# Linear attention's scores on one Trainium2 core: high and low key parts stacked on the rows, two products in place of three

## The chip, the cores and the metric

One core of a Trainium2 chip runs the whole program. The metric is the device time of one execution in microseconds (us), lower is better. TensorE does the matrix products, VectorE (DVE), ScalarE (ACT) and GpSimd (POOL) the work on elements, and SyncE (SP) issues the transfers.

## What is computed

A two-layer encoder on 512 tokens of 1024 channels, all in 32-bit floats. A layer normalizes the stream, projects it once, feeds three mixers (attention, a long convolution, gated linear attention), merges them with gates, and adds a cross-attention and an MLP. The change touches the linear attention alone: four heads, keys and queries of 64 channels, values of 128, one scan forward and one backward. The part of the reference that matters:

```
q_dec = q * jnp.exp(b)
a = jnp.einsum("bhncd,bhnsd->bhncs", q_dec, k * jnp.exp(-b))
mask = jnp.tril(jnp.ones((C, C), dtype=bool), k=0 if include_diag else -1)
o = jnp.einsum("bhncs,bhnse->bhnce", jnp.where(mask, a, 0.0), v)
...
o_f = gla_scan(q, k, v, g_f, True)
o_b = fl(gla_scan(fl(q), fl(k), fl(v), fl(g_b), False))
```

The scores `a` of both directions are what the change computes in another way.

## The kernel before, in words

**Products in three parts.** TensorE takes its operands in a rounded 32-bit format (F32R). To keep precision, `split` (L234 to L237) makes of every operand a high part, by a cast on ScalarE (L235), and a low part, by a subtraction on VectorE (L236); `mm3` (L249 to L253) then adds three products into one accumulator: high by high (L251), high by low (L252), low by high (L253).

**Layout of the heads.** For each head, one tile `qd` and one tile `kd` of 128 rows by 512 tokens hold the decayed queries and keys: rows 0 to 63 are the forward direction, rows 64 to 127 the backward one. They come from `gla_proj`, and `gla_heads` (L997) works through the heads in order, in three steps for each: the scores; the states; the output.

**The scores.** `gla_heads` splits `qd` and `kd` (two casts of 128x512 on ScalarE, two subtractions on VectorE), takes for each direction `d` the row half `rr`, and for each of four tiles of 128 tokens calls `mm3` on 64 rows: keys are the weights, queries move. That is 3 x 4 x 2 = 24 products a head, each with 64 rows of weights and 128 columns. The two directions use opposite halves of the rows of the array and write two accumulators. Direction 0 is then copied to `A` by ScalarE (L1019), direction 1 laid over it under a mask by VectorE (L1021).

**Order.** The text of the program is woven from generators by a list of step names (`ORDER0`, `ORDER`); each instruction has a priority by its place there, and `late("gA")` sets the score products back by 100. A planner then fixes the order on every engine before the run, with buffers handed out from pools (`g`: 13 in this phase, `st`: 6). So between the score products of a head there can stand products of other work: wide ones (128x512) of the projections, and transposes.

**Names in the rows.** `qdh`, `qdl`, `kdh`, `kdl` are the high and low parts; `ps` is an accumulator; `Ah`, `Sh` scores and states; `osq` squares of a head's output; `wh`, `wl`, `xh`, `xl` weights and stream of the projections. In the changed kernel the stacked tiles are named `k2` and `q2`, which lists show as `k` and `q`.

Of the kernel before, what the change touches and what calls it, by code (L numbers as in the profile page):

```python
# [10 lines left out]
F32 = mybir.dt.float32  # L11
F32R = mybir.dt.float32r
# [3 lines left out]
ALU = mybir.AluOpType  # L16
# [158 lines left out]
class Trunk:  # L175
# [821 lines left out]
    def gla_heads(self, l):  # L997
        nc, W = self.nc, self.I["w_in"][l]
        self.yc = []
        for h in range(4):  # L1000
# [1 line left out]
            tiles = lambda ap: ap.rearrange("p (t s) -> p t s", s=P)  # L1002
            per_tile = lambda ap: ap.unsqueeze(2).to_broadcast([P, NT, P])
            qh, ql = self.split_new(self.qd[h], "g", name="qd")
            kh, kl = self.split_new(self.kd[h], "g", name="kd")
            vh, vl = self.split_new(self.vf[h], "g", (P, NT, P), "v", lo_eng=nc.gpsimd)
            k3 = self.t("st", name="k3")
            nc.gpsimd.tensor_tensor(tiles(k3), tiles(self.kd[h]), per_tile(end), op=ALU.mult)
# [2 lines left out]
            for d in range(2):  # L1011
                rr = slice(64 * d, 64 * d + 64)
                ps = self.ps("a", (P, NT, P))
                for t in range(NT):
                    tk = slice(t * P, (t + 1) * P)
                    with self.late("gA"):
                        self.mm3(ps[:, t], kh[rr, tk], kl[rr, tk], qh[rr, tk], ql[rr, tk], True, True)
                if d == 0:
                    nc.scalar.copy(A, ps)  # L1019
                else:  # L1020
                    nc.vector.copy_predicated(A, self.mask.unsqueeze(1).to_broadcast([P, NT, P]), ps)  # L1021
# [3 lines left out]
            ps = self.ps("a", (P, NT, P))  # L1025
# [37 lines left out]
            for t in range(NT):  # L1063
                tk = slice(t * P, (t + 1) * P)
# [399 lines left out]
```

## Time and profile before

| what | value |
|---|---|
| median of 3 runs | 2220.78 us (2219.13 to 2222.26) |
| the profiled execution's own time | 2222.39 us |
| its span | 2220.6 us |
| TensorE busy | 2176.5 us, 98% of the span |
| VectorE, ScalarE, GpSimd busy | 68%, 46%, 9% |
| granted TensorE clock, mean | 0.992 of full speed |
| score products | 192 of 10968 TensorE products |

The busy time of TensorE is a union of overlapping records (a product's record is longer than the step to the next), so what one product takes is read from the starts in the timeline. Around the span lie 1.8 us of the execution.

### The profile page before, as it was taken

To read this page: it belongs to the slowest core of one execution; us is meant where nothing else is said; L and a number is where in the kernel's file an instruction comes from. 1 tells how busy PE (TensorE), PEld (TensorE's weight loads), DVE (VectorE), ACT (ScalarE), POOL (GpSimd) and SP (SyncE) were. 2 spreads that over 40 slices of the span, in tenths; PEclk is the share of its full clock that TensorE was granted. 3 is DMA by queue.
4 is the path that set the end of the run, shared out by engine and by line. 5 is a ranking of instruction groups with operands and counts; after the bars stand their busy time and mean duration, and the time that the engine had idled before them with its cause. 6 is when DMAs were issued, how large, how long until landed. Compare 5 with 4: busy or idle time off the path is not lost.

```text
span 2220.6 us, 28780 instructions
## 1 busy us (share of the span) xinstructions
PE 2176.5 (98%) x10968; PEld 1822.2 (82%) x10968; DVE 1517.3 (68%) x2539; ACT 1015.9 (46%) x1711; POOL 203.3 (9%) x193
## 2 busy tenths in 40 slices
PE   7999999999999999999999999999999999999999
PEld 5878888888788878888887978888887888888887
DVE  7699955869866756776485686657897575344445
ACT  6666845433344544443336477453434454332231
POOL 2030001000010200000060130100000101000004
PEclk9999999999999999999999999999999999999999
DMA  6442123233243333333344311342233312333332
GB/s 234 147 135 88 65 77 119 60 102 114 86 137 101 95 110 121 125 117 95 97 166 131 109 57 47 97 128 76 81 110 124 133 58 86 95 96 104 95 99 92
DMA packets 80098, 233.56 MB, mean 105 GB/s; under 512 B 9174, under 2 KB 11222, under 8 KB 79960
## 3 DMA queue, kind: packets, MB, share of 16 engines
q1 hardware_dynamic: 76792, 225.95, 31.9%
q0 software_dynamic: 3168, 5.77, 1.0%
q8 instruction: 86, 1.41, 0.3%
q14 instruction: 52, 0.43, 0.1%
HBM read 214.91 MB, written 16.78 MB: 104 GB/s over the span
## 4 chain that ended last, share of the span: by engine, by line
PE 75%; DVE 3%; ACT 2%; DMA 1%; issue 1%; POOL 0%; ACTq 0%; DVEq 0%; POOLq 0%
PE ps L251 24%; PE ps L253 24%; PE ps L252 24%; DVE wl L236 1%; ACT wh L235 1%; DMA wr<-in_w_in_dram 1%; PE ps L1318 0%; PE ps L555 0%; PE ps L793 0%; PE ps L543 0%; PE ps L564 0%; ACT p L547 0%; ACT pth L235 0%; PE ps L1276 0%; DVE ab L966 0%
## 5 line engine op out<-in xcount | busy, mean ns | idle before, releaser
L236 DVE TENSOR_TENSOR wl<-wr,wh 128x1024 fp32r<-128x1024 f32 x324 | 402.3, 1243 | 265.8 <-ACT wh L235 258.5
L235 ACT CAST wh<-wr 128x1024 fp32r<-128x1024 f32 (+1 forms) x328 | 341.6, 1043 | 512.1 <-PE ps L252 413.4
L253 PE MATMUL ps<-xh,wl 128*128 128x512 f32 x1344 | 530.9, 396 | 9.0 <-DVE wl L236 9.0
L251 PE MATMUL ps<-xh,wh 128*128 128x512 f32 x1344 | 533.3, 397 | 2.0 <-ACT wh L235 1.6
L252 PE MATMUL ps<-xl,wh 128*128 128x512 f32 x1344 | 529.4, 394 | 0.0
L253 PEld LDWEIGHTS ps<-xh,wl 128*128 128x128 f32 x1344 | 254.9, 190 | 63.9 <-DVE wl L236 12.3
L251 PEld LDWEIGHTS ps<-xh,wh 128*128 128x128 f32 x1344 | 254.7, 190 | 56.6 <-ACT wh L235 2.9
L252 PEld LDWEIGHTS ps<-xl,wh 128*128 128x128 f32 x1344 | 254.8, 190 | 49.7
L253 PE MATMUL ps<-hdh,wl 128*128 128x512 f32 x512 | 199.4, 390 | 0.0
L252 PE MATMUL ps<-hdl,wh 128*128 128x512 f32 x512 | 199.4, 390 | 0.0
L251 PE MATMUL ps<-hdh,wh 128*128 128x512 f32 x512 | 199.2, 389 | 0.0
L1380 DVE TENSOR_TENSOR macc<-ps,macc 128x512 f32<-128x512 f32 x96 | 66.3, 690 | 85.4 <-PE ps L253 84.8
L253 PEld LDWEIGHTS ps<-hdh,wl 128*128 128x128 f32 x512 | 96.1, 188 | 19.9
L251 PEld LDWEIGHTS ps<-hdh,wh 128*128 128x128 f32 x512 | 96.1, 188 | 19.8
L252 PEld LDWEIGHTS ps<-hdl,wh 128*128 128x128 f32 x512 | 96.1, 188 | 19.8
L352 POOL TENSOR_TENSOR hsum<-hsum,hsq 128x512 f32<-128x512 f32 x30 | 43.4, 1446 | 582.9 <-ACT hsq L350 582.9
L252 PE MATMUL ps<-wl,xh 128*128 128x256 f32 x320 | 91.6, 286 | 1.0 <-DVE wl L236 0.9
L251 PE MATMUL ps<-wh,xh 128*128 128x256 f32 x320 | 91.5, 286 | 0.1
L253 PE MATMUL ps<-wh,xl 128*128 128x256 f32 x320 | 90.9, 284 | 0.0
L1364 DVE TENSOR_TENSOR rl<-rl 128x512 f32<-128x512 f32 x64 | 44.0, 688 | 63.4 <-ACT rl L1363 63.4
L1382 POOL TENSOR_TENSOR macc<-macc,rb 128x512 f32<-128x512 f32 x16 | 23.5, 1469 | 651.2 <-DVE macc L1380 651.2
L1363 ACT ACTIVATE rl<-ps 128x512 f32<-128x512 f32 x64 | 37.9, 592 | 77.9 <-PE ps L253 77.9
(403 smaller groups left out, 4309.1 us busy)
## 6 DMA issues: line engine op xcount, KB each, us to landing
wr<-in_mlp_w_dram SPq DMA_DIRECT2D x128, 512.0 KB, 3.6
wr<-in_w_in_dram SPq DMA_DIRECT2D x108, 512.0 KB, 3.7
wraw<-in_x_wv_dram SPq DMA_DIRECT2D x16, 512.0 KB, 5.5
wr<-in_x_wk_dram SPq DMA_DIRECT2D x16, 512.0 KB, 3.6
F<-ff SPq DMA_DIRECT2D x32, 256.0 KB, 2.9
F<-F SPq DMA_DIRECT2D x32, 256.0 KB, 4.8
wr<-in_w_out_dram SPq DMA_DIRECT2D x16, 512.0 KB, 3.6
wr<-in_x_wq_dram SPq DMA_DIRECT2D x16, 512.0 KB, 3.7
```

The costliest lines, as they stand in the source:

```text
L235: r = self.nc.scalar.copy(hi, src)
L236: (lo_eng or self.nc.vector).tensor_tensor(lo, src, hi, op=ALU.subtract)
L251: mm(out, lh, rh, start=start, stop=False, skip_group_check=True)
L252: mm(out, lh, rl, start=False, stop=False, skip_group_check=True)
L253: mm(out, ll, rh, start=False, stop=stop, skip_group_check=True)
L352: eng.tensor_tensor(self.hsum, self.hsum, sq, op=ALU.add)
L1363: nc.scalar.activation(r, ps, AF.Relu)
L1364: nc.vector.tensor_tensor(r, r, r, op=ALU.mult)
L1380: nc.vector.tensor_tensor(acc[m], ps, acc[m], op=ALU.add)
L1382: nc.gpsimd.tensor_tensor(acc[m], acc[m], rb, op=ALU.mult)
```

## The change

For each head and each direction `d`, a tile `kk` of 128 rows is made: the rows of the direction (`r`) hold the high part of the keys, the other half (`o`) their low part. A tile `qq` holds the high part of the queries twice, once in each half. One product of 128 rows then gives high by high plus low by high; a second product, of the 64 rows `r` alone, adds high keys by low queries. The queries' own split is kept, since their parts are used again behind.

On ScalarE the one cast of the keys (128x512) becomes, for each direction, one cast of 64x512 for the keys and two of 64x512 for the queries' copies; on VectorE the one subtraction (128x512) becomes two of 64x512. The tiles `kk` take the two `g` buffers of the old parts; the tiles `qq` take two more `st` buffers a head.

```diff
--- before.py
+++ after.py
@@ -1002,7 +1002,18 @@
             tiles = lambda ap: ap.rearrange("p (t s) -> p t s", s=P)
             per_tile = lambda ap: ap.unsqueeze(2).to_broadcast([P, NT, P])
             qh, ql = self.split_new(self.qd[h], "g", name="qd")
-            kh, kl = self.split_new(self.kd[h], "g", name="kd")
+            kd, K2, Q2 = self.kd[h], [], []
+            for d in range(2):
+
+                r, o = slice(64 * d, 64 * d + 64), slice(64 - 64 * d, 128 - 64 * d)
+                kk = self.t("g", dt=F32R, name="k2")
+                nc.scalar.copy(kk[r], kd[r])
+                nc.vector.tensor_tensor(kk[o], kd[r], kk[r], op=ALU.subtract)
+                K2.append(kk)
+                qq = self.t("st", dt=F32R, name="q2")
+                for x in (r, o):
+                    nc.scalar.copy(qq[x], qh[r].bitcast(F32))
+                Q2.append(qq)
             vh, vl = self.split_new(self.vf[h], "g", (P, NT, P), "v", lo_eng=nc.gpsimd)
             k3 = self.t("st", name="k3")
             nc.gpsimd.tensor_tensor(tiles(k3), tiles(self.kd[h]), per_tile(end), op=ALU.mult)
@@ -1014,7 +1025,10 @@
                 for t in range(NT):
                     tk = slice(t * P, (t + 1) * P)
                     with self.late("gA"):
-                        self.mm3(ps[:, t], kh[rr, tk], kl[rr, tk], qh[rr, tk], ql[rr, tk], True, True)
+                        nc.tensor.matmul(ps[:, t], K2[d][:, tk], Q2[d][:, tk], start=True, stop=False,
+                                         skip_group_check=True)
+                        nc.tensor.matmul(ps[:, t], K2[d][rr, tk], ql[rr, tk], start=False, stop=True,
+                                         skip_group_check=True)
                 if d == 0:
                     nc.scalar.copy(A, ps)
                 else:
```

Three places in the planned order. The first is TensorE, scores of head 2 in layer 0, before (`qdh`/`qdl` with `kdh`/`kdl`: 64 rows each; `ps_3558` is direction 0, on the first half of the rows, `ps_3572` direction 1, on the second):

```order
L1087 MATMUL ps_3533<-consts,oy_3528 128x128
L251 MATMUL ps_3558<-qdh_3543,kdh_3547 128x128
L252 MATMUL ps_3558<-qdl_3544,kdh_3547 128x128
L251 MATMUL ps_3572<-qdh_3543,kdh_3547 128x128
L253 MATMUL ps_3558<-qdh_3543,kdl_3548 128x128
L251 MATMUL ps_3558<-qdh_3543,kdh_3547 128x128
L252 MATMUL ps_3558<-qdl_3544,kdh_3547 128x128
L252 MATMUL ps_3572<-qdl_3544,kdh_3547 128x128
L253 MATMUL ps_3558<-qdh_3543,kdl_3548 128x128
L251 MATMUL ps_3558<-qdh_3543,kdh_3547 128x128
L252 MATMUL ps_3558<-qdl_3544,kdh_3547 128x128
```

and of the change (L1028 is the stacked product, 128 rows; L1030 the second one, 64 rows):

```order
L1101 MATMUL ps_3533<-consts,oy_3528 128x128
L1028 MATMUL ps_3566<-q_674_3550,k_673_3547 128x128
L1030 MATMUL ps_3566<-qdl_3544,k_673_3547 128x128
L1028 MATMUL ps_3566<-q_674_3550,k_673_3547 128x128
L1028 MATMUL ps_3576<-q_676_3556,k_675_3553 128x128
L1030 MATMUL ps_3566<-qdl_3544,k_673_3547 128x128
L1028 MATMUL ps_3566<-q_674_3550,k_673_3547 128x128
L1030 MATMUL ps_3566<-qdl_3544,k_673_3547 128x128
L1028 MATMUL ps_3566<-q_674_3550,k_673_3547 128x128
L1030 MATMUL ps_3566<-qdl_3544,k_673_3547 128x128
L1030 MATMUL ps_3576<-qdl_3544,k_675_3553 128x128
L1028 MATMUL ps_3576<-q_676_3556,k_675_3553 128x128
```

Before, all 24 products of this head stand together and have 64 rows; now products of 128 and of 64 rows take turns. Counted over the eight groups of scores in the order of TensorE, the height changes 36 times before (8, 2, 2, 4, 10, 4, 2, 4 times, entry and exit of a group included) and 114 times now (14 times in each group, 16 in one).

The second place is ScalarE at the split of head 1 in layer 0 (`A` is the copy of the scores), before:

```order
L235 CAST Sh_3231<-S_3208 128x512
L235 CAST qdh_3327<-qk_100_522 128x512
L235 CAST kdh_3331<-qk_115_694 128x512
L235 CAST vh_3335<-vf_2879 128x512
L1073 ACTIVATE osq_3322,small<-ps_3297 128x128 x4
L1019 COPY A_3341<-ps_3342 128x512
```

and of the change:

```order
L235 CAST Sh_3231<-S_3208 128x512
L235 CAST qdh_3327<-qk_100_522 128x512
L1010 CAST k_638_3331<-qk_115_694 64x512
L1010 CAST k_640_3337<-qk_115_694 64x512
L235 CAST vh_3343<-vf_2879 128x512
L1087 ACTIVATE osq_3322,small<-ps_3297 128x128 x4
L1015 CAST q_639_3334<-qdh_3327 64x512 x2
L1015 CAST q_641_3340<-qdh_3327 64x512 x2
L1033 COPY A_3349<-ps_3350 128x512
```

The copies of the queries stand behind the squares of head 0's output now. On TensorE the scores of head 1, which stood ahead of all but one of that output's products, now stand behind them and ten wide products more. In layer 1 the copies stand behind the squares too, and the scores behind ten wide products.

The third place is VectorE where head 0 of layer 1 is prepared, before:

```order
L236 TENSOR_TENSOR qdl_12299<-qk_1693_10387,qdh_12298 128x512
L973 TENSOR_TENSOR ab_11134<-ab_11134,small 128x512
L236 TENSOR_TENSOR kdl_12303<-qk_1699_10455,kdh_12302 128x512
L531 TENSOR_TENSOR ql_11162<-ps_11156,qh_11161 64x512
L982 SCALAR_TENSOR_TENSOR qk_1697_10421<-qk_1697_10421,mn_11153 128x512
```

and of the change:

```order
L236 TENSOR_TENSOR qdl_12299<-qk_1701_10387,qdh_12298 128x512
L973 TENSOR_TENSOR ab_11134<-ab_11134,small 128x512
L1011 TENSOR_TENSOR k_2012_12302<-qk_1707_10455,k_2012_12302 64x512
L1011 TENSOR_TENSOR k_2014_12308<-qk_1707_10455,k_2014_12308 64x512
L531 TENSOR_TENSOR ql_11162<-ps_11156,qh_11161 64x512
```

One more subtraction stands ahead of the attention's `ql`.

## Rows read from the trace of the kernel before

**Rows 1.** The page, parts 1 and 4: busy time of each engine with its share of the span and its count of instructions; and the chain that ended last, by engine.

```profile
PE 2176.5 (98%) x10968; PEld 1822.2 (82%) x10968; DVE 1517.3 (68%) x2539; ACT 1015.9 (46%) x1711; POOL 203.3 (9%) x193
...
PE 75%; DVE 3%; ACT 2%; DMA 1%; issue 1%; POOL 0%; ACTq 0%; DVEq 0%; POOLq 0%
```

**Rows 2.** The groups of TensorE instructions by line and form: the first of the three groups of score products (the other two, on L252 and L253, have the same 64 instructions and form). Columns: line, engine, operation, tiles, weights' rows*columns, moving rows x columns, count | busy us, mean ns of one | idle us before.

```profile
L251 PE MATMUL ps<-qdh,kdh 64*128 64x128 f32 x64 | 15.3, 294 | 0.7 <-ACT kdh L235 0.7
```

**Rows 3.** The timeline of TensorE in layer 0, the scores of head 2, with transposes of other work ahead and behind. Columns: start us, duration us, engine, line, operation, tiles, form, count of merged instructions. 'x2' is two products whose starts fall together, one of each half of the rows.

```profile
382.65 0.60 PE L1087 MATMUL ps<-consts,oy 128*128 128x128 f32 x4
383.17 0.33 PE L251 MATMUL ps<-qdh,kdh 64*128 64x128 f32 x2
383.34 0.33 PE L252 MATMUL ps<-qdl,kdh 64*128 64x128 f32 x2
383.45 0.27 PE L253 MATMUL ps<-qdh,kdl 64*128 64x128 f32 x1
383.56 0.27 PE L251 MATMUL ps<-qdh,kdh 64*128 64x128 f32 x1
...
384.12 0.33 PE L253 MATMUL ps<-qdh,kdl 64*128 64x128 f32 x2
384.23 0.33 PE L251 MATMUL ps<-qdh,kdh 64*128 64x128 f32 x2
384.34 0.33 PE L252 MATMUL ps<-qdl,kdh 64*128 64x128 f32 x2
384.46 0.33 PE L253 MATMUL ps<-qdh,kdl 64*128 64x128 f32 x2
...
385.19 0.27 PE L253 MATMUL ps<-qdh,kdl 64*128 64x128 f32 x1
385.39 0.44 PE L1028 MATMUL ps<-consts,k 128*128 128x128 f32 x2
```

**Rows 4.** The same view in layer 1, the scores of head 0, with wide products (128x512) of other work between them.

```profile
1391.30 0.39 PE L251 MATMUL ps<-wh,mnh 128*128 128x512 f32 x1
1391.52 0.39 PE L252 MATMUL ps<-wl,mnh 128*128 128x512 f32 x1
1391.84 0.32 PE L251 MATMUL ps<-qdh,kdh 64*128 64x128 f32 x1
1392.09 0.50 PE L253 MATMUL ps<-wh,mnl 128*128 128x512 f32 x1
1392.53 0.33 PE L251 MATMUL ps<-qdh,kdh 64*128 64x128 f32 x1
1392.78 0.66 PE L1028 MATMUL ps<-consts,k 128*128 128x128 f32 x4
...
1393.95 0.50 PE L251 MATMUL ps<-wh,mnh 128*128 128x512 f32 x1
1394.38 0.32 PE L253 MATMUL ps<-qdh,kdl 64*128 64x128 f32 x1
1394.55 0.27 PE L251 MATMUL ps<-qdh,kdh 64*128 64x128 f32 x1
```

**Rows 5.** Busy time by stretch: from:to, its length, busy us and count of each engine, then the granted TensorE clock (1.00 is 2.4 GHz, 0.50 is 1.2 GHz), the DMA share and GB/s. The first row spans the scores of head 0 of layer 0; the third begins inside those of head 1.

```profile
301.30:306.00 4.70, 4.70 (x32) 3.69 (x31) 1.82 (x2) 2.16 (x3) 0.00 (x0) 1.00 0.59 197
306.00:309.40 3.40, 3.40 (x9) 2.72 (x9) 2.32 (x5) 1.10 (x2) 0.00 (x0) 0.50 0.11 41
...
326.50:336.70 10.20, 10.20 (x48) 9.49 (x47) 0.19 (x1) 1.84 (x10) 1.32 (x2) 0.50 0.01 2
...
383.00:1302.70 919.70, 909.86 (x4480) 759.46 (x4478) 649.91 (x1083) 400.36 (x627) 91.72 (x82) 1.00 0.35 111
...
1309.50:2214.00 904.50, 901.08 (x4496) 754.09 (x4495) 567.88 (x883) 371.49 (x626) 62.30 (x46) 1.00 0.30 94
```

**Rows 6.** The timeline of TensorE behind the scores of head 0, layer 0: two wide products in a row.

```profile
307.02 0.63 PE L253 MATMUL ps<-xh,wl 128*128 128x512 f32 x1
307.45 0.63 PE L251 MATMUL ps<-xh,wh 128*128 128x512 f32 x1
```

**Rows 7.** Groups of ScalarE instructions by line and form, columns as in Rows 2: the keys' high part now, and a cast of 64 rows of 512 from the same memory.

```profile
L533 ACT CAST ql<-ql 64x512 fp32r<-64x512 f32 x16 | 9.9, 618 | 0.8 <-DVE ql L531 0.3
...
L235 ACT CAST kdh<-qk 128x512 fp32r<-128x512 f32 x8 | 4.9, 616 | 0.0
```

**Rows 8.** The timeline of TensorE at the scores of head 1, layer 0; in brackets the idle time before, and what ended it.

```profile
324.87 0.33 PE L251 MATMUL ps<-qdh,kdh 64*128 64x128 f32 x2 [0.73 <-ACT kdh L235]
...
325.76 0.32 PE L253 MATMUL ps<-qdh,kdl 64*128 64x128 f32 x1 [0.28 <-DVE kdl L236]
```

**Rows 9.** The timeline of ScalarE there: the squares of head 0's output (four with their sums), and the copy behind them.

```profile
334.86 0.28 ACT L1073 ACTIVATE osq<-ps 128x128 f32<-128x128 f32 x1 [9.53 <-PE ps L253]
...
335.88 0.60 ACT L1019 COPY A<-ps 128x512 f32<-128x512 f32 x1
```

**Rows 10.** The timeline of TensorE where head 0 of layer 1 is prepared: the longest single wait in that stretch.

```profile
1303.97 1.22 PE L543 MATMUL ps<-k,ql 128*128 128x512 f32 x2 [3.29 <-ACT ql L533]
```

**Rows 11.** The timeline of VectorE there: the keys' low part, and the low part of the attention's queries behind it.

```profile
1301.87 0.68 DVE L236 TENSOR_TENSOR kdl<-qk,kdh 128x512 fp32r<-128x512 f32 x1
1302.59 0.68 DVE L531 TENSOR_TENSOR ql<-ps,qh 64x512 fp32r<-64x512 f32 x1
```

**Rows 12.** Busy time by stretch, columns as in Rows 5: where head 0 of layer 0 is prepared.

```profile
140.00:180.00 40.00, 36.69 (x168) 29.79 (x167) 39.60 (x77) 22.12 (x41) 11.40 (x14) 0.97 0.39 123
```


## The prediction, as it was made before the changed kernel ran

> **What bounds the kernel now.** I read the page first: TensorE is busy 98% of the span and is 75% of the chain that ended last, every other engine far behind [rows 1]. So what lengthens or shortens TensorE's own line of work goes nearly whole into the time, and what the other engines get added costs only where TensorE waits for them. The page counts records that overlap, so the price of a product is not its mean of 294 ns [rows 2] but the step from its start to the next start, and that is in the timeline.
>
> Three things are to be seen in the scores of one head [rows 3]. Within a run of 64-row products the step is 0.11 us (383.45 to 383.56). Where "x2" stands, two products start together, one on each half of the rows: their line holds two products in a step of 0.11. And from the last 64-row product to the first 128-row one the step is 0.20 us (385.19 to 385.39), with no wait named: 0.09 is lost on the way out. The other way it is the same, and the first step after a change is 0.16 to 0.17 in place of 0.11 (383.17 to 383.34; 1394.38 to 1394.55) [rows 3, 4]. So a run of products of one height costs 0.11 for each, and 0.05 at its beginning and 0.09 at its end: **0.14 us for each change of height**. A product alone between two changes shows it at once: 0.25 us, 1391.84 to 1392.09 and 1392.53 to 1392.78 [rows 4]. A wide product alone between two changes takes 0.44 and 0.43, and 0.22 in a run (1391.30 to 1391.52): 0.2 on top [rows 4].
>
> **The products themselves.** Three groups of 64 [rows 2] become two: 64 products fewer, at 0.11 a step, -7.0 us.
>
> **The changes of height.** The stacked product has 128 rows, the one after it 64, and the planned order lets them take turns: 114 changes for 36, 78 more at 0.14, +10.9 us.
>
> **The shared time.** A 128-row product uses both halves, so it cannot start together with another. In the group of head 2 that is lost: 24 products at 0.11, plus 0.14 for the two changes' parts that lie within, would be 2.78 us, and from 383.17 to 385.39 it takes 2.22 [rows 3], 0.56 less. I take 0.5 for each of eight groups, +4.0 us. Back comes what the order still leaves: in most groups one 64-row product of each direction stands side by side, 0.11 each, -0.9 us.
>
> Together +7.0 us on TensorE. As a whole: now 192 x 0.11 - 4.0 + 36 x 0.14 = 22.2 us, then 128 x 0.11 - 0.9 + 114 x 0.14 = 29.1 us, or 2.8 and 3.6 us a head. No row shows a 128-row product of 128 columns alone between two changes. From above it is bounded by the wide one, which pays 0.2 where the narrow 64-row one pays 0.14 [rows 4]: 0.06 more for six or so a head, eight heads, +2.9 us, so 9.9. From below, a change could cost nothing in the new order: then 14.1 us in place of 22.2, -8.1. I take 0.14, since it is the row of the nearest form, the same columns and the same two changes.
>
> The Trainium skill has a rule on each side. TensorEngine Tiling (Array Packing), section Key Properties, says that changing the tiling mode, not just the tile, drains TensorE; it gives no price, and the trace agrees, with 0.20 in place of 0.11 at each change. TensorE: Matmul & The Clock Gate, section LDWEIGHTS (loading the stationary operand), says that a weight load goes by its columns and that a 32-row one takes as long as a 128-row one. By that rule alone rows are free, and the change is a gain of its 64 products; it stands beside the first rival below.
>
> **The clock.** The granted clock is 0.50 right behind the scores of head 0 in layer 0, for 3.4 us, and again from within those of head 1, for 10.2 us [rows 5]; at that level a wide product takes 0.43 in place of 0.22 [rows 6], so half of each stretch is lost: 6.8 us of the 13.6. It stays at 1.00 for all other groups (the long stretches from 383.0 and from 1309.5) [rows 5]. Both falls came at groups that were broken up by changes or held up by waits [rows 5, 8]; one more group as broken up, that of head 0 in layer 1 [rows 4], had none: two of three. Every group is broken up like that after the change and lasts 3.6 us, so I take falls at six of eight, 3.4 us each: 20.4 us at half clock for 13.6, +3.4 us. The ends: none at all, -6.8; all eight, one of them as long as now, 34.0 for 13.6, +10.2.
>
> **ScalarE and VectorE.** One cast of 616 ns becomes six of 64x512, and a cast of that form takes 618 [rows 7], so rows don't shorten it: 40 more in all, 25 us on an engine that is free for half of the span [rows 1]. They are hidden wherever a split stands well ahead of its scores, which is so for all heads but head 1. There TensorE now waits 0.73 us for a cast and 0.28 for a subtraction [rows 8]. The new order moves these scores behind head 0's output, which takes that wait away, -1.0 us. But the copies of the queries stand behind the squares, which take 1.0 us from 334.86 to 335.88 [rows 9], and two casts are 1.2 more, while TensorE has ten wide products, 2.2 us, to do meanwhile. That is even; with the hand-over from engine to engine, which is not in it, I put 0.3 us of wait in both layers, +0.6. In layer 1, TensorE waits 3.29 us for the attention's `ql` [rows 10], whose subtraction follows the keys' low part on VectorE at once [rows 11]. Two subtractions of 64 rows stand there now; these take 0.68 each (a 64-row one is the row of `ql` itself), so the wait grows by 0.6 us. Where head 0 of layer 0 is split, VectorE is busy 39.60 of 40 us and TensorE only 36.69 [rows 12], so one more subtraction is worth up to 0.6 there too. Sum +0.8; between -1.0, if none of the waits comes, and +3, if all casts of head 1 hold TensorE up. No transfer is added or moved past another by the change itself; the two more `st` buffers a head are used and free again within a head. The planner also reorders rows elsewhere; I price that at nothing and allow 3 us each way, about the longest single wait that I cite.
>
> **The sum.** 7.0 + 3.4 + 0.8 = +11.2 us. On the profiled execution's 2222.39 that is 2233.6; that execution lies 1.6 above the median of the runs shown, 2220.78, against which I forecast **2232.0 us**, slower by 0.5%. With the bounds of each part its own range is 2226 to 2241.
>
> **The rivals.**
> First, the change of height is paid for only by what stands now, where products of other work come between, and is hidden when the same accumulator goes on: the next weights load behind the product that runs. For it: steps of 0.11 within a run hide the loads already [rows 3]. Against it: the same 0.20 stands at every change, between all kinds of neighbours [rows 3, 4]. Then the scores take 14.1 us, -8.1, with the waits' +0.8 and the clock as now: 2213.5 us, **faster**. It decides at 0.08 us a change: there 128 x 0.11 - 0.9 + 114 x 0.08 is the 22.2 of now. Chance 0.14. In the Trainium skill, the columns-only rule of TensorE: Matmul & The Clock Gate, cited above, speaks for this rival.
> Second, the falls of the clock go away, since half of the products now fill all 128 rows: 7.0 - 6.8 + 0.8 = +1.0, 2221.8 us, **no difference**. For it: six of eight groups have no fall now [rows 5]. Against it: the groups get longer and more broken up. Chance 0.16.
> Third, the casts become the bound: at head 1 of both layers TensorE waits for five more casts, 3.1 us each at 0.62 [rows 7], 6.2 us for the 0.6 above: 2237.6 us. It would be seen as a wait for a cast ahead of the first stacked product. Against it: ten wide products stand between. Chance 0.08.
>
> **How the numbers follow.** The forecast has 0.62. What a measurement of this kernel can tell from no change is about 0.2%, 4.4 us. Slower by more: forecast and third rival, 0.70. Within: the second, 0.16. Faster by more: the first, 0.14. The range runs from 2219, which takes in the second rival with 3 us for the order elsewhere, to 2241; it leaves out the first rival and a little at the top.
>
> **What would show it.** In the profile after: stacked and 64-row products in turn with steps of 0.25 us, no "x2" but for side-by-side 64-row ones; 3.6 us from the first to the last of a group; a granted clock of 0.50 right behind most groups; the wait of 0.73 at head 1 gone and the wait for `ql` at some 3.9 us. Wrong would be steps of 0.11 across the two forms (the first rival), or no stretch at 0.50 between 300 and 420 us (the second). More than 1 us of wait ahead of a stacked product would speak for the third.

## The result, and the profile of the changed kernel

The changed kernel takes 2238.52 us (median of four runs, 2236.58 to 2243.68), the kernel before beside it 2220.94. The ratio is 1.0085, with a 95% interval of 1.0071 to 1.0099: slower by 17.6 us, 0.8%. The forecast was 2232.0 in a range of 2219 to 2241. The profiled execution took 2238.0 us, its span is 2236.2: 15.6 longer than the span before.

The page, parts 1 and 4, answers to [rows 1]. TensorE has 64 products fewer and is busy 10.8 us longer; the chain is still its own line of work.

```profile
PE 2187.3 (98%) x10904; PEld 1827.4 (82%) x10904; DVE 1528.3 (68%) x2547; ACT 1041.7 (47%) x1751; POOL 199.0 (9%) x193
...
PE 87%; DVE 6%; ACT 4%; DMA 1%; issue 1%; POOL 0%; SPq 0%; ACTq 0%; DVEq 0%; POOLq 0%
```

The groups of score products by line and form answer to [rows 2]: columns as there. The means, 317 and 331 ns, are again lengths of overlapping records; that they rose by a tenth says little beside the steps that follow.

```profile
L1028 PE MATMUL ps<-q,k 128*128 128x128 f32 x64 | 19.3, 317 | 0.3 <-ACT q L1015 0.3
L1030 PE MATMUL ps<-qdl,k 64*128 64x128 f32 x64 | 18.9, 331 | 0.0
```

The timeline of TensorE at the scores of head 2 in layer 0 answers to [rows 3]: start us, duration us, engine, line, tiles, form, count of merged instructions.

```profile
382.39 0.30 PE L1028 MATMUL ps<-q,k 128*128 128x128 f32 x1
382.62 0.32 PE L1030 MATMUL ps<-qdl,k 64*128 64x128 f32 x1
382.87 0.44 PE L1028 MATMUL ps<-q,k 128*128 128x128 f32 x2
383.24 0.32 PE L1030 MATMUL ps<-qdl,k 64*128 64x128 f32 x1
383.50 0.33 PE L1028 MATMUL ps<-q,k 128*128 128x128 f32 x1
383.75 0.32 PE L1030 MATMUL ps<-qdl,k 64*128 64x128 f32 x1
384.00 0.33 PE L1028 MATMUL ps<-q,k 128*128 128x128 f32 x1
384.26 0.33 PE L1030 MATMUL ps<-qdl,k 64*128 64x128 f32 x2
384.52 0.33 PE L1028 MATMUL ps<-q,k 128*128 128x128 f32 x1
...
385.81 0.32 PE L1030 MATMUL ps<-qdl,k 64*128 64x128 f32 x1
386.06 0.33 PE L1042 MATMUL ps<-consts,k 128*128 128x128 f32 x1
```

Read the starts: 383.24, 383.50, 383.75, 384.00, 384.26, 384.52. Each product, of 128 rows or of 64, takes 0.25 to 0.26 us, though none waits; before, the step was 0.11. Where two of one kind follow each other (x2 at 382.87), they take 0.37 together, 0.12 more than one; the x2 at 384.26 is a pair of opposite halves and costs no more than one product. The group takes 3.67 us (382.39 to 386.06) for 16 products, where 24 took 2.22.

Busy time by stretch answers to [rows 5]: from:to, length, busy us and count of PE, PEld, DVE, ACT, POOL, then the granted clock (1.00 is 2.4 GHz, 0.50 is 1.2), DMA share, GB/s.

```profile
302.20:306.00 3.80, 3.80 (x21) 2.70 (x19) 1.82 (x2) 2.11 (x3) 0.00 (x0) 0.99 0.57 161
306.00:309.40 3.40, 3.40 (x9) 2.71 (x9) 2.16 (x4) 1.10 (x2) 0.00 (x0) 0.50 0.34 134
326.40:329.80 3.40, 3.40 (x12) 2.82 (x12) 0.99 (x2) 3.15 (x12) 2.50 (x2) 0.51 0.00 0
...
411.80:415.20 3.40, 3.40 (x15) 3.17 (x16) 2.50 (x4) 1.41 (x3) 0.00 (x0) 0.50 0.00 0
...
1401.60:1405.00 3.40, 3.40 (x10) 2.62 (x9) 1.86 (x5) 1.10 (x2) 0.00 (x0) 0.51 0.15 61
...
1428.90:1435.70 6.80, 6.80 (x17) 5.30 (x17) 2.32 (x5) 1.10 (x2) 0.00 (x0) 0.50 0.13 51
...
1514.30:1517.70 3.40, 3.40 (x16) 3.21 (x16) 3.24 (x6) 1.69 (x3) 0.00 (x0) 0.50 0.00 0
```

The first two rows are one event: a group of alternating products, TensorE busy without a gap and at 0.99, and then 3.4 us at 0.50. Five of the eight groups are followed by such a stretch, one of them of 6.8 us. The row at 326.40 stands just ahead of the scores of head 1.

The timeline of TensorE at its waits answers to [rows 8, 10]; brackets give the idle time and what ended it.

```profile
324.71 0.33 PE L251 MATMUL ps<-Sh,qdh 128*128 128x128 f32 x1 [0.78 <-ACT Sh L235]
325.44 0.33 PE L252 MATMUL ps<-Sl,qdh 128*128 128x128 f32 x1 [0.40 <-DVE Sl L236]
...
330.66 0.22 PE L1028 MATMUL ps<-q,k 128*128 128x128 f32 x1
...
1303.87 0.73 PE L542 MATMUL ps<-k,qh 128*128 128x512 f32 x2 [1.89 <-ACT qh L530]
...
1309.22 1.03 PE L543 MATMUL ps<-k,ql 128*128 128x512 f32 x2 [3.02 <-ACT ql L533]
```

The first scores of head 1 start without a wait (330.66), but the waits they had, 0.73 and 0.28, now stand ahead of head 0's output, whose products take the early place: 0.78 and 0.40. In layer 1 a wait of 1.89 us is new. The timeline of ScalarE shows what the attention's `qh` stood behind: a step (L975) that itself waited 1.13 us for VectorE, and the two casts of the keys, 1.25.

```profile
1300.17 0.63 ACT L975 ACTIVATE mn<-ab 128x512 f32<-128x512 f32 x1 [1.13 <-DVE ab L973]
...
1301.38 1.25 ACT L1010 CAST k<-qk 64x512 fp32r<-64x512 f32 x2
1302.65 1.17 ACT L530 CAST qh<-ps 64x512 fp32r<-64x512 f32 x2
```

### The profile page after: what moved, and what is told of

It is laid out like the page before. It is cut to its first block, busy times and chain, and to the rows that moved or that the text cites. A ratio compares the mean times of both kernels' runs of the same rounds, so it can differ in the third digit from the quotient of the medians.

```text
span 2236.2 us, 28707 instructions
## 1 busy us (share of the span) xinstructions
PE 2187.3 (98%) x10904; PEld 1827.4 (82%) x10904; DVE 1528.3 (68%) x2547; ACT 1041.7 (47%) x1751; POOL 199.0 (9%) x193
## 4 chain that ended last, share of the span: by engine, by line
PE 87%; DVE 6%; ACT 4%; DMA 1%; issue 1%; POOL 0%; SPq 0%; ACTq 0%; DVEq 0%; POOLq 0%
PE ps L251 27%; PE ps L252 27%; PE ps L253 27%; DVE wl L236 1%; DMA wr<-in_w_in_dram 1%; ACT wh L235 1%; PE ps L555 1%; ACT p L547 1%; PE ps L1030 1%; PE ps L1028 1%; PE ps L564 1%; PE ps L542 0%; ACT pth L235 0%; PE ps L566 0%; PE ps L543 0%
## 5 line engine op out<-in xcount | busy, mean ns | idle before, releaser
L253 PE MATMUL ps<-xh,wl 128*128 128x512 f32 x1344 | 530.7, 395 | 7.3 <-DVE wl L236 7.3
L252 PE MATMUL ps<-xl,wh 128*128 128x512 f32 x1344 | 529.5, 395 | 0.0
L253 PEld LDWEIGHTS ps<-xh,wl 128*128 128x128 f32 x1344 | 254.8, 190 | 62.0 <-DVE wl L236 10.3
L252 PEld LDWEIGHTS ps<-xl,wh 128*128 128x128 f32 x1344 | 255.1, 190 | 50.4
L253 PE MATMUL ps<-hdh,wl 128*128 128x512 f32 x512 | 199.6, 390 | 0.0
L252 PE MATMUL ps<-hdl,wh 128*128 128x512 f32 x512 | 199.6, 390 | 0.0
L253 PEld LDWEIGHTS ps<-hdh,wl 128*128 128x128 f32 x512 | 96.2, 188 | 19.8
L252 PEld LDWEIGHTS ps<-hdl,wh 128*128 128x128 f32 x512 | 96.2, 188 | 19.7
L252 PE MATMUL ps<-wl,xh 128*128 128x256 f32 x320 | 91.4, 286 | 0.4 <-DVE wl L236 0.4
L253 PE MATMUL ps<-wh,xl 128*128 128x256 f32 x320 | 91.4, 286 | 0.0
L1378 DVE TENSOR_TENSOR rl<-rl 128x512 f32<-128x512 f32 x64 | 44.1, 688 | 62.4 <-ACT rl L1377 62.4
```

The costliest lines, as they stand in the source:

```text
L252: mm(out, lh, rl, start=False, stop=False, skip_group_check=True)
L253: mm(out, ll, rh, start=False, stop=stop, skip_group_check=True)
L1378: nc.vector.tensor_tensor(r, r, r, op=ALU.mult)
```

## The experiments

For every profiled execution I take the span apart in the same way. *Idle* is the span less TensorE's busy time. *Half clock* is the sum of all stretches at 0.50 up to TensorE's last product, of which I take half as lost. What is left, the *rest*, holds the score products (all else is the same work), and is given as the difference to before. Beside it stands what the prediction's two prices give: 0.11 us a step, 0.14 a change of height. For the change the sum closes: +15.6 = 4.8 idle + 1.7 clock + 9.1 rest.

| kernel | median us | ratio to before (95%) | idle us | half clock us | changes of height | rest us | by the two prices |
|---|---|---|---|---|---|---|---|
| before | 2220.94 | 1 | 44.1 | 37.5 | 36 | 0 | 0 |
| the change | 2238.52 | 1.0085 (1.0071 to 1.0099) | 48.9 | 41.0 | 114 | +9.1 | +7.0 |
| e1 heights apart | 2225.64 | 1.0025 (1.0014 to 1.0037) | 54.6 | 30.7 | 26 | -4.1 | -8.0 |
| e2 halves paired | 2213.84 | 0.9964 (0.9949 to 0.9978) | 47.9 | 23.9 | 18 | -9.2 | -9.1 |
| e4 all of 128 rows | 2218.04 | 0.9988 (0.9978 to 0.9997) | 51.5 | 23.9 | 0 | -6.4 | -8.1 |
| e5 late pairs | 2246.93 | 1.0117 (1.0100 to 1.0134) | 46.4 | 75.1 | 118 | +5.2 | +7.7 |
| e3 casts alone | 2230.24 | 1.0049 (1.0034 to 1.0064) | 49.7 | 37.5 | 40 | +1.8 | +0.6 |
| e7 before, early | 2227.01 | 1.0036 (1.0024 to 1.0047) | 48.0 | 51.2 | 18 | -4.5 | -2.6 |
| e8 change, early | 2243.78 | 1.0110 (1.0091 to 1.0129) | 49.2 | 51.2 | 116 | +5.9 | +7.2 |
| e9 no copies | 2239.45 | 1.0082 (1.0062 to 1.0102) | 46.3 | 58.0 | 112 | +3.7 | +6.7 |
| e10 pairs in place | 2217.26 | 0.9990 (0.9980 to 0.9999) | 49.6 | 30.7 | 20 | -10.3 | -8.8 |

Each ratio is against runs of the kernel before on the same chip. The three columns in us are each of one execution, and the clock scatters most between executions. The mean granted clock of each execution was taken, too; 1 less that clock, times the span, estimates what the clock costs. For the change this is 24.6 us on average (four executions, 22.4 to 29.1), for the kernel before 16.0 to 17.4 (13 to 23 executions on each of three chips). By this estimate the clock is about 7 us of the change's 17.6, and not 1.7, and idle time and rest together are about 11, not 13.9.

My theory: the change of height costs, and takes more than the saved products give. Rivals: the 128-row form itself is dear, the casts are, or the place of the scores in the order is.

**e1: the same products, sorted by height.** All eight stacked products of a head first, then the eight of 64 rows, halves in turn, and the group kept together.

```diff
-            for d in range(2):
-                rr = slice(64 * d, 64 * d + 64)
-                ps = self.ps("a", (P, NT, P))
+            pss = [self.ps("a", (P, NT, P)) for d in range(2)]
+            with self.tc.high_priority(offset=1000):
+                for d in range(2):
...
+                        nc.tensor.matmul(pss[d][:, t], K2[d][:, tk], Q2[d][:, tk], start=t == 0, stop=False, ...)
...
+                    for d in range(2):
+                        rr = slice(64 * d, 64 * d + 64)
+                        nc.tensor.matmul(pss[d][:, t], K2[d][rr, tk], ql[rr, tk], start=False, stop=t == NT - 1, ...)
```

> The change's casts, tiles and products, in another order: for a head all eight stacked products first, then the eight 64-row ones with the two halves of the rows in turn, and high priority so that they stay together. 26 changes of height in the planned order in place of 114. Theory (each change of height costs 0.14 us on TensorE): 10.6 us of steps + 26 x 0.14 = 14.2 us for all scores in place of 29.1, so 15 us under the change: some 2223, and less if falls of the clock behind the groups go away too (down to 2213). Rival (the added casts and the waits they bring are the cost, changes of height are free): no other than the change, 2238 within 3.

The timeline of TensorE at one head:

```profile
378.35 1.09 PE L1027 MATMUL ps<-q,k 128*128 128x128 f32 x8
379.37 0.66 PE L1033 MATMUL ps<-qdl,k 64*128 64x128 f32 x8
379.96 0.33 PE L1047 MATMUL ps<-consts,k 128*128 128x128 f32 x1
```

The 16 products that took 3.67 us take 1.61, so neither form is dear in itself; only their taking turns is. The rest fell by 13.2 us against the change (15.0 by the prices: some groups kept waits and foreign products within them), and the whole by less, as TensorE idles 5.7 us more. The place was changed along with the sorting; e8 below tells these apart.

**e4: the change with no change of height.** The low queries too are copied into both halves, so the second product has 128 rows (high and low keys by low queries), at the price of four more subtractions a head.

```diff
+                ll = self.t("st", dt=F32R, name="l2")
+                for x in (r, o):
+                    nc.vector.tensor_tensor(ll[x], self.qd[h][r], qh[r], op=ALU.subtract)
+                L2.append(ll)
...
-                        nc.tensor.matmul(ps[:, t], K2[d][rr, tk], ql[rr, tk], start=False, stop=True,
+                        nc.tensor.matmul(ps[:, t], K2[d][:, tk], L2[d][:, tk], start=False, stop=True,
```

> The change in its own loop order, but the second product has 128 rows too: the low part of the queries is laid in both halves as well (four more 64x512 subtractions a head on VectorE), so the product adds low by low to what is asked for. As many products as the change, no change of height. Theory: 128 x 0.11 = 14.1 us for the scores in place of 29.1: 15 us under the change, 2223, some 1 to 3 us more for the subtractions, less for falls of the clock that go away. Rival (casts and their waits): 2238 or above, as more is added.

The same view of head 2:

```profile
373.54 0.28 PE L1034 MATMUL ps<-l,k 128*128 128x128 f32 x1
373.65 0.28 PE L1032 MATMUL ps<-q,k 128*128 128x128 f32 x1
373.76 0.27 PE L1034 MATMUL ps<-l,k 128*128 128x128 f32 x1
```

This is the cleanest trial: the same number of products as the change, more rows in half of them, more work on VectorE, and steps of 0.11 in place of 0.25. The rest is -6.4 us where the prices say -8.1, and the time 20.5 us under the change: of the 21.4 us of span between the two profiles, 15.5 are the rest and 8.5 the clock, and idle time takes 2.6 back. The priority of the products was left as it is; the planner still moved them in places (13 products of other work stand within the group of head 3 in layer 0, where the change has 4). The Trainium skill, TensorE: Matmul & The Clock Gate, section LDWEIGHTS (loading the stationary operand), says that rows don't matter to a weight load; these steps agree with it, within one height.

**e2: the old products, opposite halves side by side.** Before's 24 products and its split, the two directions in turn, kept together.

```diff
+            pss = [self.ps("a", (P, NT, P)) for d in range(2)]
+            with self.tc.high_priority(offset=1000):
...
+                    for i, (kx, qx) in enumerate(((kh, qh), (kh, ql), (kl, qh))):
+                        for d in range(2):
+                            rr = slice(64 * d, 64 * d + 64)
+                            nc.tensor.matmul(pss[d][:, t], kx[rr, tk], qx[rr, tk], start=i == 0, stop=i == 2, ...)
```

> The kernel before with its own 24 products of 64 rows a head, ordered so that direction 0 and direction 1 always follow each other, kept together by high priority: 18 changes of height (36 before). Theory: 96 shared steps x 0.11 + 18 x 0.14 = 13.1 us in place of 22.2, 9 us under the kernel before: 2212, and down to 2205 if the falls of the clock at the groups go. If products of opposite halves did not really run side by side: no more than the 18 changes, 2.5 us, so 2218.

The same view:

```profile
375.19 0.28 PE L1018 MATMUL ps<-qdl,kdh 64*128 64x128 f32 x2
375.31 0.27 PE L1018 MATMUL ps<-qdh,kdl 64*128 64x128 f32 x2
375.42 0.28 PE L1018 MATMUL ps<-qdh,kdh 64*128 64x128 f32 x2
...
1291.84 0.47 PE L1018 MATMUL ps<-qdl,kdh 64*128 64x128 f32 x2 [3.88 <-DVE qdl L236]
```

Every line of head 2 is a pair, and the steps are 0.12 and 0.11: 24 products in 1.48 us, against 2.22 in [rows 3]. Two products of opposite halves cost one. It is the fastest version that ran, 0.36% under before. Its early place makes TensorE wait 3.88 us for head 0 of layer 1, with the clock at 0.50 behind that wait. This is no loss against before: the wait of 3.29 for the attention's `ql` [rows 10] is gone from that stretch, and before, too, stood at 0.50 there for 6.8 us (1302.7 to 1309.5).

**e5: the same pairs, late.** The priority of e2 replaced by the one that before and the change use, so that wide products of other work come between.

```diff
-            with self.tc.high_priority(offset=1000):
+            with self.late("gA"):
```

> The products and tiles of the run with paired halves, but with the low priority of the kernel before: the planner then puts wide products between the pairs of the first head of each layer, 118 changes of height in place of 18. No cast or tile is added to the kernel before. Theory (change of height): 100 changes more at 0.14 to 0.2 us, 14 to 20 us above the run with paired halves, 2 to 8 us above the kernel before. Rival (changes of height are free, casts cost): the same time as the run with paired halves, within 2 us.

The timeline of TensorE at head 0, at full and at half clock, and the stretches at half clock:

```profile
303.09 0.50 PE L252 MATMUL ps<-xl,wh 128*128 128x512 f32 x1
303.52 0.33 PE L1018 MATMUL ps<-qdl,kdh 64*128 64x128 f32 x1
303.78 0.51 PE L253 MATMUL ps<-xh,wl 128*128 128x512 f32 x1
...
310.12 0.47 PE L1018 MATMUL ps<-qdh,kdh 64*128 64x128 f32 x1
310.52 0.79 PE L253 MATMUL ps<-xh,wl 128*128 128x512 f32 x1
311.25 0.47 PE L1018 MATMUL ps<-qdh,kdh 64*128 64x128 f32 x1
...
309.10:326.10 17.00, 17.00 (x33) 9.55 (x34) 1.46 (x3) 2.18 (x4) 0.00 (x0) 0.50 0.00 0
1408.20:1428.70 20.50, 20.50 (x44) 11.68 (x44) 2.03 (x3) 3.62 (x8) 0.00 (x0) 0.50 0.12 45
```

Here no product has the stacked form, there is no added cast, and yet this is the slowest kernel: 26 us above before, where I had put 2 to 8. The wide products stand between the two halves of a pair, too, so a 64-row product and a wide one take turns, 0.69 us for both (303.09 to 303.78, next wide product) in place of 0.33. That is 118 changes of height and 25 steps more than in e2, +7.7 by the prices; the rest is +5.2 us.

The clock gives +18.8 more by the table's rule. The stretches of 17.0 and 20.5 us begin within the groups of head 0, which start at 301.3 and 1403.2, and outlast them: the turns go on until 322.9 and 1425.4. At half clock two products in turn take 1.13 us (310.12 to 311.25), less than twice 0.69, so some 3 us of the 18.8 belong to the rest (an estimate from these two steps). So turns of height cost with other products than the change's, too; but most of the loss here is the clock, which the two prices don't hold.

**e3: the change's casts, before's products.** Keys cast and subtracted in halves, the four copies made and not used, `mm3` on 64 rows kept.

```diff
+            kh, kl = (self.t("g", dt=F32R, name="k2") for _ in range(2))
...
+                nc.scalar.copy(kh[r], kd[r])
+                nc.vector.tensor_tensor(kl[r], kd[r], kh[r], op=ALU.subtract)
...
+                        self.mm3(ps[:, t], kh[rr, tk], kl[rr, tk], qh[rr, tk], ql[rr, tk], True, True)
```

> The change's work on the other engines, without its products: six casts and three subtractions a head as in the change (the high parts of the keys by halves, the copies of the queries, which nothing reads here), the two more st buffers a head, and then the 24 products of 64 rows of the kernel before. 40 changes of height in the planned order (36 before). Theory (changes of height cost, casts are hidden): the kernel before and the 0.8 us of waits and 0.6 of changes, 2220 to 2224. Rival (the casts and their waits are most of the 17.6 us): 2232 or above.

The timeline of TensorE at head 1 of layer 0, and the clock behind it:

```profile
323.71 0.32 PE L251 MATMUL ps<-qdh,k 64*128 64x128 f32 x1 [1.93 <-ACT k L1009]
...
324.50:338.10 13.60, 13.60 (x52) 11.75 (x52) 3.06 (x7) 5.50 (x16) 2.37 (x2) 0.50 0.00 1
```

My theory missed: I had put 2220 to 2224, and it is 11 us slower than before with almost the same steps. The scores of head 1 stand directly behind the key casts here, the waits of 0.73 and 0.28 [rows 8] become one of 1.93, and 13.6 us at half clock follow, for 10.2 in [rows 5]. The table puts 5.6 of its 7.4 us of span into idle time. Of these, 0.9 are that wait, and 2.7 stand between 138 and 300 us, where layer 0 is prepared: TensorE idles 7.9 us there for 5.2 before. So the casts and subtractions are not free; in the change they are hidden at head 1, since its scores start without a wait (330.66 above), but not between 138 and 300 us, where it idles 7.8.

**e9: the change without the copies.** `Q2` is `qh` itself, so 32 casts and the two `st` buffers a head fall away. Left out is the copy of the high queries into the other half, so the stacked product multiplies the low keys by the other direction's queries.

```diff
-                qq = self.t("st", dt=F32R, name="q2")
-                for x in (r, o):
-                    nc.scalar.copy(qq[x], qh[r].bitcast(F32))
-                Q2.append(qq)
+                Q2.append(qh)
```

> The change without its copies of the queries: the stacked products take the high part of the queries as it lies (its other half belongs to the other direction, so the numbers are not the reference's); 32 casts of 64x512 on ScalarE and the two more st buffers a head go, all products and their turns stay: 112 changes of height. It prices the copies inside the change. By the prediction's sum the casts and subtractions are worth 0.8 us in all: 2237 to 2239. If they bring the added idle time of TensorE, 48.9 us in place of 44.1, then 3 to 6 us less than the change: 2232 to 2236. If, as the run with the casts alone (11 us over the kernel before) suggests, they are two thirds of the loss: 2228 or below.

TensorE at head 1 of layer 0, and the clock behind it:

```profile
326.62 0.33 PE L1025 MATMUL ps<-qdh,k 128*128 128x128 f32 x1 [1.68 <-DVE k L1011]
...
326.90:340.50 13.60, 13.60 (x46) 11.28 (x46) 1.11 (x2) 2.15 (x10) 2.49 (x2) 0.50 0.01 1
```

The time is that of the change within both intervals, where the prediction's sum gave 2237 to 2239: idle fell by 2.6 us and the rest by 5.4, and the clock took 8.5 back. Without copies the planner moves the scores of head 1 ahead again, right behind the subtraction of the keys, and the pattern of e3 returns. So removing the copies buys nothing net; what they cost in a fixed order, this did not show.

**e7 and e8: is it the place?** Before and the change, each with the early priority of e1 and e2 and nothing else.

```diff
-                    with self.late("gA"):
+                    with self.tc.high_priority(offset=1000):
```

> The kernel before with nothing but the high priority for its score products that the run with paired halves had: the order within a head is the old one, direction 0 ahead of direction 1 for the most part, 18 changes of height. It separates pairing from place. Theory: 192 x 0.11 - 4.0 + 18 x 0.14 = 19.6 us of scores, 6.5 us over the run with paired halves: about 2220. If the place and priority made that run fast, and not the pairs: the same as it, 2214 within 2.

> The change with the same high priority for its score products: 116 changes of height (114), stacked and 64-row products still in turn, but no longer put late between the other work. Theory: nothing gained on the scores, 29 us of them, so within 4 us of the change, 2234 to 2242. If the late place of the products, with the casts in front, were the cause: 2225 or below.

Early alone makes before slower by 0.36% (idle +3.9, half clock +13.7), 7 us above the 2220 that I had put. The change is not faster early either: 1.0110 for 1.0085, with intervals that overlap, and 2 us above what I had put. So e1 and e2 are fast in spite of their place. Between e8 and e1, the same place and the same products sorted, lie 18 us in the medians; between e7 and e2, 13. Not all of that is steps: in the profiles 10.0 of the 14.8 us of span between e8 and e1 are the rest, but only 4.7 of the 18.4 between e7 and e2, where the clock is 13.6.

**e10: the best version with its wait taken away.** e2 with a later place for the group of head 0 and the common one for the others.

```diff
-            with self.tc.high_priority(offset=1000):
+            with self.tc.high_priority(offset=0 if h else -150):
```

> The paired halves with another priority: for head 0 slightly later than the kernel before, for the others none, so that the groups stay together (20 changes of height) and head 0's scores no longer stand where its operands are not ready. The run with paired halves at high priority showed a group of 8.0 us at head 0 of layer 1, 6.5 over its other groups. Theory: 10.6 + 20 x 0.14 = 13.4 us of scores, and most of those 6.5 us back: 2207 to 2212. If the wait there is not the place's doing: 2214 as before.

TensorE in layer 1, and the clock around it:

```profile
1294.59 0.84 PE L543 MATMUL ps<-k,ql 128*128 128x512 f32 x2 [3.26 <-ACT ql L533]
...
1396.88 0.33 PE L251 MATMUL ps<-vh,kth 128*128 128x128 f32 x1 [3.71 <-ACT kth L235]
...
1393.00:1397.50 4.50, 0.79 (x5) 0.52 (x4) 3.75 (x9) 1.10 (x2) 0.00 (x0) 1.00 0.04 16
1397.50:1404.30 6.80, 6.80 (x23) 5.61 (x22) 3.24 (x10) 0.00 (x0) 0.00 (x0) 0.50 0.00 0
```

I had put 2207 to 2212, and it missed. The pairs stayed together, and the wait for `qdl` went; but the attention's wait for `ql`, which before had and e2 had not, is back in its place with 3.26, so there was little to win. And a wait of 3.71 for the states' `kth` came, with a fall of the clock behind it. e2 stays the best.

## Why the prediction was right, and where its sizes were off

The measured time lies 6.5 us above the forecast, within the stated range. The four kernels with 112 changes of height or more are the four slowest, by 8 us, as the mechanism says; the terms of the clock and of the other engines were too small. (The narrower range, 2226 to 2241, is not worked out in the prediction: laid end to end, the bounds of its parts without the first rival give 2217 to 2247.)

**The products and the changes of height** (+7.0): right in mechanism and nearly in size. The alternating step is 0.25 to 0.26 as said. It was not known whether a lone 128-row product pays 0.14 or, like the wide one, 0.2 [rows 4]: it pays 0.14. A group takes 3.6 to 3.7 us net of foreign products, as said. The rest is +9.1 in place of +7.0, inside its bounds; over the ten kernels the two prices give the rest within 4 us, from -10.3 to +9.1. The price of a change is thus shown by the steps themselves, by taking it away (e4, e1) and by making it with other products (e5).

**The shared time** (+4.0 in it): right. In e2 all products share, and 96 steps do what 192 products did; in the trace of before, the starts of the 192 products make about 156 steps, 36 of 0.11 us fewer, which is the 4.0.

**The clock** (+3.4): right in place, too small in size. Falls stand behind five groups, and one just ahead of head 1's scores, where I put six of eight. Around the scores the half-clock time is 23.8 us (five stretches of 3.4 and one of 6.8) for 13.6 [rows 5], +5.1 lost. In the profiles the net is only +1.7, since 10.2 us of half clock between 43 and 190 us are gone, and one of 3.4 came at 1695. These early falls come and go without a change of order: TensorE's order is the same in both kernels up to 159 us, and e5, where it is that of before up to 302 us, has no fall between 138 and 150 us either. The rows are of before, of the change and of e5:

```profile
138.00:150.00 12.00, 12.00 (x46) 9.71 (x47) 11.88 (x22) 5.58 (x11) 7.47 (x8) 0.86 0.43 127
138.00:150.00 12.00, 11.52 (x51) 9.20 (x50) 11.88 (x23) 7.30 (x13) 8.18 (x8) 1.00 0.43 130
138.00:150.00 12.00, 12.00 (x55) 9.86 (x54) 11.87 (x23) 4.93 (x8) 4.77 (x8) 1.00 0.41 126
```

So that they are gone here is luck, and the small net with it. Over all executions the clock costs the change about 7 us more than before (the estimate under the table), twice the +3.4.

**ScalarE and VectorE** (+0.8): this term was mis-sized; idle time grew by 4.8. The waits of 0.73 and 0.28 did go from the scores, as said, and came back as 0.78 and 0.40 for `Sh` and `Sl` of head 0, whose products took that place: a gain of 1.0 that was no gain. I named the wait for `ql` to grow from 3.29 to 3.9; it is 3.02, but 1.89 stand ahead of it for `qh`, together 4.91 for 3.29. There I had counted the subtractions on VectorE, and not that `qh` would stand behind the casts of the keys (1301.38 above) and behind a step that waits for VectorE. Yet between 1160 and 1320 us TensorE idles no longer than before (9.1 us for 9.4), as smaller waits there went. What grew most stands between 138 and 300 us, where the heads of layer 0 are prepared: 7.8 us of idle time for 5.2, where I had put up to 0.6 for one subtraction. e3 has 7.9 there with the same casts and the old products, which points to the work on the other engines, and not to the products; how much of it is scatter is not shown, since e5, without an added cast and in the order of before, has 6.6.

**The rivals.** The first (a change of height is hidden) is refuted by the steps of 0.25. The second (the falls go away) by the 0.50 rows at 306.0 and 411.8. The third (the casts bound head 1) did not happen in the change: the first stacked product waits for nothing. e3 and e9 show that it was near, since an order in which the scores follow the casts gives just that, at 1.7 to 1.9 us of wait and 13.6 us of half clock.

What stays open: which part of the idle time the casts cause in the change's own order, since every edit of them moved the order, too; which of the change's falls, beside those around the scores, make up its 7 us; and why a fall lasts 3.4 us at one place and 20.5 at another.

## What to carry to other kernels

Count changes of row height between neighbouring products before counting products: a product fewer is worth one step, and two changes cost two and a half. If products use half of the rows, put opposite halves next to each other in the order, or fill all rows in all of them; a mixture is worse than either. And when a planner orders the work, price an edit by the order that it gives as a whole: the wait that an edit removes may pass to what takes its place.

## What the runs showed of the hardware that was not expected

Two 64-row products on opposite halves start together and take one step of 0.11 us for as long as the order pairs them: in e2 twelve pairs in a row, 1.48 us for 24 products. The Trainium skill, TensorE: Matmul & The Clock Gate, section Part 3: Packing small matmuls — row/col tiling, says that products in different row groups run concurrently in the array; the trace agrees, for two halves of 64 rows.

The clock falls to 0.50 after quite different things. In the change it falls behind groups in which TensorE was busy all the time (3.80 of 3.80 us from 302.2) but alternated heights, and in e5 it stays there for 17.0 us, all of them busy, of which heights alternate for 13.8; in e10 behind a wait in which it was busy 0.79 of 4.50 us. A wait of 3.7 us there cost about 7 us, since the 6.8 at half clock behind it lost 3.4.
